# Loading a sum of positive parts over two DMA queues instead of one

## Chip, core and metric

The kernel runs on one core of a Trainium2 chip. The metric is the device time of one execution in microseconds (us), as the median of several runs. The core has the engines SyncE (SP, which issues DMAs), ScalarE (ACT), VectorE (DVE), GpSimd (POOL) and TensorE, which this kernel does not use. Data come from HBM through 16 DMA engines; a DMA instruction on an engine's own queue hands them their work.

## The reference

```python
x = randn(32, 512, 1024)            # float32, 67.1 MB
out = sum(maximum(x, 0), axis=-1)   # float32, 32 x 512
```

Each of 16,384 rows of 1024 numbers becomes one number, the sum of its positive parts. Every byte is read once and almost nothing is written.

## The kernel before

The rows are dealt to the 128 partitions. A **block** is 16 rows in each partition (128 x 16,384 floats, 8.39 MB), contiguous in HBM for each partition, so 64 KB in a piece. Seven blocks (0 to 6) go through three buffers `io0` to `io2` in turn; block 0 lies in a part of the input of its own, so that its sums can be stored early. An eighth block, the **tail**, comes in smaller and smaller loads: 8 rows, 4 rows, 2302 numbers ("head"), 873, 518 and 403 numbers, each partition. Before, all loads are issued by SyncE on its queue, by `load` (line 103). One load has one semaphore of its own, which counts 16 when it has landed.

Two ways of computing a row are used. For most blocks ScalarE clamps the whole block or half of it in place (`clamp`, line 144) and VectorE then reduces it along the last axis (`total`, line 152); `TWO` lists how many rows are taken at a time: 16 in blocks 0 and 1, twice 8 in blocks 2 to 4, twice 7 in block 5. The other rows are done alone, clamp and sum in one instruction with an accumulator, on ScalarE (`act_row`, line 159) or VectorE (`dve_row`, line 167); block 6 has eight of each, and the tail is done this way too, with the last two rows cut into parts (`act_part`, line 121, `dve_part`, line 126, a clamp on GpSimd, line 234, and a last joining instruction on VectorE, line 254).

The order on each engine is the order in which the program writes it; there is no scheduler. The first three loads wait for nothing. The load of block j from 3 on, and the first of the tail, waits until VectorE's count says that the block three before it, in the same buffer, has been read:

```python
loaded = load(buf[:, :, :], rows(m, ROWS), j >= NBUF and freed[j - NBUF])
```

`freed[j]` holds the counts of ScalarE and VectorE when block j is done; the load waits for VectorE's, which ends last. ScalarE's first instruction of block 0 is the load of its function table (line 142), which waits for block 0, and then the clamp. The three stores (line 115) are issued by SyncE behind all loads.

`open_without_barrier` takes the barrier out of the program's opening and puts the first load (`EARLY = 1`) ahead of the engine's first branch, so that it is issued at once.

Of the kernel before, what the change touches and what calls it, by code (L numbers as in the profile page):

```python
# [5 lines left out]
RELU = mybir.ActivationFunctionType.Relu  # L6
# [3 lines left out]
ROWS = 16  # L10
NBUF = 3
# [19 lines left out]
def kernel(tc: tile.TileContext, x: bass.AP, out: bass.AP):  # L31
    nc = tc.nc
    sems = Semaphores(tc)

    tc.close()
    tc.compile()
    nc.cur_bb = nc.bb_map[tc.start_bb_name]
    body = nc.cur_bb.bb.instructions
    ends = list(body)
    body.clear()  # L40
    n_stores = relu_sum(nc, sems, x, out)
    body.extend(ends)


    nc.cur_bb = nc.bb_map[tc.start_bb_name + "_end"]
    nc.cur_bb.bb.instructions.clear()
    nums = sorted(s.num for s in (*sems.loads, sems.act, sems.dve))
    cleared = range(nums[0], nums[-1] + 1)
    assert len(cleared) == len(nums)
    nc.sync.sem_clear(cleared)  # L50
    nc.sync.wait_ge(sems.stored, 16 * n_stores).then_inc(sems.stored, -16 * n_stores)
    open_without_barrier(tc, EARLY)
# [12 lines left out]
def relu_sum(nc, sems: Semaphores, x: bass.AP, out: bass.AP):  # L65
# [3 lines left out]
    NB = len(TWO)  # L69
# [4 lines left out]
    bufs = [nc.alloc_sbuf_tensor(f"io{i}", [P, ROWS, D], F32) for i in range(NBUF)]  # L74
    res = nc.alloc_sbuf_tensor("res", [P, NT], F32)
# [13 lines left out]
    def rows(m, n):  # L89
        if m < ROWS:  # L90
            return xf[:, m : m + n, :]
        return xv[:, m - ROWS : m - ROWS + n, :]
# [5 lines left out]

    n_load = n_act = n_dve = n_store = 0

    def load(dst, src, after=None):
        nonlocal n_load
        dma = nc.sync.dma_start(out=dst, in_=src)  # L103
        if after:
            dma.wait_op(sems.dve, after[1], "sem-ge")
        dma.then_inc(sems.loads[n_load], 16)
        n_load += 1
        return sems.loads[n_load - 1]

    def store(m, n, act, sem, count):  # L110
        nonlocal n_store
        dst, src = sums(m, n)
        if act:
            nc.sync.wait_ge(sems.act, act)
        nc.sync.dma_start(out=dst, in_=src).wait_op(sem, count, "sem-ge").then_inc(
            sems.stored, 16
        )
        n_store += 1
# [20 lines left out]
    def clamp(ap, loaded):  # L139
        nonlocal n_act  # L140
        if n_act == 0:
            nc.scalar.preload_act_table(RELU).wait_op(loaded, 16, "sem-ge")  # L142
            loaded = None
        i = nc.scalar.activation(out=ap, in_=ap, func=RELU)  # L144
        if loaded is not None:
            i.wait_op(loaded, 16, "sem-ge")
        i.then_inc(sems.act, 1)
        n_act += 1

    def total(ap, m, n):  # L150
        nonlocal n_dve
        nc.vector.tensor_reduce(  # L152
            out=res[:, m : m + n], in_=ap, axis=mybir.AxisListType.X, op=ADD
        ).wait_op(sems.act, n_act, "sem-ge").then_inc(sems.dve, 1)
        n_dve += 1

    def act_row(ap, accum_out, loaded):
        nonlocal n_act
        i = nc.scalar.activation(out=ap, in_=ap, func=RELU, accum_out=accum_out)  # L159
        if loaded is not None:  # L160
            i.wait_op(loaded, 16, "sem-ge")
        i.then_inc(sems.act, 1)
        n_act += 1

    def dve_row(ap, accum_out, loaded):
        nonlocal n_dve
        i = nc.vector.tensor_scalar(  # L167
            out=ap,
            in0=ap,
            scalar1=0.0,  # L170
            scalar2=None,
            op0=MAX,
            op1=ADD,
            accum_out=accum_out,
        )
        if loaded is not None:
            i.wait_op(loaded, 16, "sem-ge")
        i.then_inc(sems.dve, 1)
        n_dve += 1

    freed = []
    m = 0
    for j in range(NB):
        buf = bufs[j % NBUF]
        loaded = load(buf[:, :, :], rows(m, ROWS), j >= NBUF and freed[j - NBUF])
        c = 0
        act_waits = dve_waits = loaded
        for n in TWO[j]:
            clamp(buf[:, c : c + n, :], act_waits)
            total(buf[:, c : c + n, :], m + c, n)  # L190
            act_waits = None
            c += n
        for _ in range(ACT[j]):
            act_row(buf[:, c, :], res[:, m + c : m + c + 1], act_waits)
            act_waits = None
            c += 1
        for _ in range(DVE[j]):
            dve_row(buf[:, c, :], res[:, m + c : m + c + 1], dve_waits)
            dve_waits = None
            c += 1  # L200
        assert c == ROWS
        freed.append((n_act, n_dve))
        m += ROWS


    buf = bufs[NB % NBUF]
    c = 0
    for n in TAIL:
        loaded = load(
            buf[:, c : c + n, :], rows(m, n), None if c else freed[NB - NBUF]  # L210
        )
        for i in range(n):
            if i % 2 == 0 or (n == 8 and i == 7):
                act_row(buf[:, c, :], res[:, m : m + 1], loaded if i == 0 else None)
            else:
                dve_row(buf[:, c, :], res[:, m : m + 1], loaded if i == 1 else None)
            c += 1
            m += 1

    flat = buf[:, :, :].rearrange("p c d -> p (c d)")  # L220
    src = rows(m, 4).rearrange("p c d -> p (c d)")
    at = c * D
# [3 lines left out]


    loaded = load(flat[:, at : at + head], src[:, :head])
    act_row(buf[:, c, :], res[:, m : m + 1], loaded)
    sums_act = n_act  # L230
    dve_row(buf[:, c + 1, :], res[:, m + 1 : m + 2], loaded)
    sums_dve = n_dve
    clamped = flat[:, at + 2 * D : at + head]
    nc.gpsimd.tensor_scalar(  # L234
        out=clamped, in0=clamped, scalar1=0.0, scalar2=None, op0=MAX
    ).wait_op(loaded, 16, "sem-ge").then_inc(sems.end, 1)
    for lo, hi, n, first, second in (
# [3 lines left out]
        loaded = load(flat[:, at + lo : at + hi], src[:, lo:hi])  # L241
        act_part(flat[:, at + lo : at + lo + n], last[:, first : first + 1], (loaded, 16))
        dve_part(flat[:, at + lo + n : at + hi], last[:, second : second + 1], (loaded, 16))
    loaded = load(last[:, 2 : 2 + n_last], src[:, middle:end])
# [10 lines left out]
        out=clamped,  # L255
# [5 lines left out]
        accum_out=res[:, NT - 2 : NT - 1],  # L261
# [6 lines left out]
def open_without_barrier(tc: tile.TileContext, n_loads: int):  # L268

    SP = mybir.EngineType.SP
    blocks = tc.nc.main_func.blocks
    opening = blocks[0].instructions
    body = next(b for b in blocks if b.name == tc.start_bb_name).instructions
    for i in list(opening):
        if isinstance(i, (mybir.InstDrain, mybir.InstEventSemaphore)):
            opening.remove(i)
    loads = [i for i in body if i.engine == SP][:n_loads]
    for i in loads:  # L280
        assert isinstance(i, mybir.InstDMACopy)
        body.remove(i)
    at = next(n for n, i in enumerate(opening) if i.engine == SP)
    opening[at:at] = loads


# [28 lines left out]
```

## Time and profile before

| | before |
|---|---|
| median of 3 runs | 160.91 us (160.89 to 160.95) |
| span of the profiled execution, first to last instruction | 159.7 us |
| left around the span (median less span) | 1.2 us |
| VectorE busy | 118.8 us, 74% |
| ScalarE busy | 103.6 us, 65% |
| HBM read | 67.11 MB, 421 GB/s over the span |
| DMA queue's share of the 16 engines' time | 98.0% |

The whole time of the profiled execution isn't listed apart from the runs; its span is set beside their median. All windows and starts are counted from the span's start, which here is SyncE's first DMA instruction. In the timeline a line has start, length, engine, line of the program, operation, output and input, how many, and in brackets how long the engine was idle before it and what ended that. An engine's wait for `DMA io<-in_x_dram` ends when a load has landed, so the start of the first clamp of a block is the landing of that block, to within some hundredths of a microsecond. The chain of waits is followed back from the last instruction, at each step to what released it.

### The profile page before, as it was taken

Reading aid. Unit: us, or ns where it says so; the run is one execution under the profiler, and the core shown is the slowest. Engines: PE = TensorE matmul, PEld = TensorE weight load, DVE = VectorE, ACT = ScalarE, POOL = GpSimd, SP = SyncE. Lnnn points to the kernel's source line nnn. Section 1 sums busy time; section 2 is a strip of 40 time slices with the busy share of each in tenths; the row PEclk is TensorE's granted clock in tenths of the full one; section 3 lists DMA queues with packets and bytes.
Section 4 is the critical chain, followed back from the end, with each engine's and each line's share of the span. In section 5 each row is a group of like instructions: output and inputs, shape, how many; then the busy total and the mean of one; then the engine's idle time right before and its main releaser. Section 6 shows DMA issues by size and latency. Waiting matters only on the chain.

```text
span 159.7 us, 125 instructions
## 1 busy us (share of the span) xinstructions
DVE 118.8 (74%) x44; ACT 103.6 (65%) x53; POOL 1.0 (1%) x5
## 2 busy tenths in 40 slices
DVE  0000000006999799999999999999999799999986
ACT  0000049993699808996099951999329993496995
POOL 0000000000000000000000000000000000000001
DMA  7996996996997997979969969969969969898993
GB/s 263 525 525 263 525 509 279 525 509 279 525 476 312 525 443 345 525 328 460 525 279 509 525 263 525 525 263 525 509 279 525 492 295 525 353 435 386 407 409 128
DMA packets 2304, 67.18 MB, mean 421 GB/s; under 512 B 640, under 2 KB 768, under 8 KB 1024
## 3 DMA queue, kind: packets, MB, share of 16 engines
q1 hardware_dynamic: 2304, 67.18, 98.0%
HBM read 67.11 MB, written 0.07 MB: 421 GB/s over the span
## 4 chain that ended last, share of the span: by engine, by line
DVE 45%; DMA 45%; ACT 9%; SPq 1%; issue 0%
DMA io<-in_x_dram 45%; DVE res L152 43%; ACT io L144 9%; DVE io L167 1%; SPq L103 1%; DVE io L126 1%; DVE io L254 0%
## 5 line engine op out<-in xcount | busy, mean ns | idle before, releaser
L152 DVE TENSOR_REDUCE res<-io 128x8 f32<-128x8192 f32 (+2 forms) x10 | 101.1, 10175 | 38.9 <-ACT io L144 38.9
L144 ACT ACTIVATE io<-io 128x8192 f32<-128x8192 f32 (+2 forms) x10 | 81.8, 8218 | 25.9 <-DMA io<-in_x_dram 25.9
L159 ACT ACTIVATE io<-io 128x1024 f32<-128x1024 f32 x18 | 18.8, 1043 | 6.6 <-DMA io<-in_x_dram 6.6
L167 DVE TENSOR_SCALAR_CACHE_REDUCE io<-io 128x1024 f32<-128x1024 f32 x14 | 16.2, 1214 | 0.5 <-DMA io<-in_x_dram 0.4
L142 ACT ACT_TABLE_LOAD x1 | 1.3, 1283 | 22.0 <-DMA io<-in_x_dram 22.0
L159 ACT ACTIVATION_READ_ACCUMULATOR io<-io 128x1 f32 x18 | 3.4, 187 | 0.0
L234 POOL TENSOR_SCALAR io<-io 128x254 f32<-128x254 f32 x1 | 0.8, 840 | 155.1 <-DMA io<-in_x_dram 155.1
L167 DVE DVE_READ_ACCUMULATOR io<-io 128x1 f32 x14 | 1.1, 82 | 0.0
L126 DVE TENSOR_SCALAR_CACHE_REDUCE io<-io 128x552 f32<-128x552 f32 (+1 forms) x2 | 1.1, 596 | 0.0
L121 ACT ACTIVATE io<-io 128x321 f32<-128x321 f32 (+1 forms) x2 | 0.9, 426 | 0.1
L254 DVE SCALAR_TENSOR_TENSOR io<-last,io 128x254 f32<-128x254 f32 x1 | 0.4, 425 | 0.0
L121 ACT ACTIVATION_READ_ACCUMULATOR io<-io 128x1 f32 x2 | 0.4, 187 | 0.0
L121 ACT ACTIVATE last<-last 128x153 f32<-128x153 f32 x1 | 0.3, 332 | 0.0
L121 ACT ACTIVATION_READ_ACCUMULATOR last<-last 128x1 f32 x1 | 0.2, 187 | 0.0
L126 DVE DVE_READ_ACCUMULATOR io<-io 128x1 f32 x2 | 0.2, 84 | 0.0
L299 POOL MEMSET const-bfloat16-1.0<- 128x1 bf16 x1 | 0.1, 101 | 0.0
L299 POOL MEMSET const-uint8-127<- 128x1 uint8 x1 | 0.1, 101 | 0.0
L299 POOL MEMSET const-float32-0.0<- 128x1 f32 x1 | 0.1, 99 | 0.2 <-issue 0.2
L299 POOL MEMSET const-float32-1.0<- 128x1 f32 x1 | 0.1, 98 | 0.0
L254 DVE DVE_READ_ACCUMULATOR io<-last,io 128x1 f32 x1 | 0.1, 83 | 0.0
## 6 DMA issues: line engine op xcount, KB each, us to landing
io<-in_x_dram SPq DMA_DIRECT2D x1, 4096.0 KB, 23.8
io<-in_x_dram SPq DMA_DIRECT2D x1, 2048.0 KB, 28.3
io<-in_x_dram SPq DMA_DIRECT2D x1, 1151.0 KB, 30.6
io<-in_x_dram SPq DMA_DIRECT2D x1, 436.5 KB, 31.2
io<-in_x_dram SPq DMA_DIRECT2D x1, 259.0 KB, 31.4
last<-in_x_dram SPq DMA_DIRECT2D x1, 201.5 KB, 31.4
io<-in_x_dram SPq DMA_DIRECT2D x7, 29.1
out_dram<-res SPq DMA_DIRECT2D x1, 55.0 KB, 1.6
```

The lines of the kernel that those rows point to most:

```text
L103: dma = nc.sync.dma_start(out=dst, in_=src)
L121: nc.scalar.activation(out=ap, in_=ap, func=RELU, accum_out=accum_out).wait_op(*after, "sem-ge").then_inc(sems.end, 1)
L126: i = nc.vector.tensor_scalar(out=ap, in0=ap, scalar1=0.0, scalar2=None, op0=MAX, op1=ADD, accum_out=accum_out,)
L142: nc.scalar.preload_act_table(RELU).wait_op(loaded, 16, "sem-ge")
L144: i = nc.scalar.activation(out=ap, in_=ap, func=RELU)
L152: nc.vector.tensor_reduce(out=res[:, m : m + n], in_=ap, axis=mybir.AxisListType.X, op=ADD).wait_op(sems.act, n_act, "sem-ge").then_inc(se ...
L159: i = nc.scalar.activation(out=ap, in_=ap, func=RELU, accum_out=accum_out)
L167: i = nc.vector.tensor_scalar(out=ap, in0=ap, scalar1=0.0, scalar2=None, op0=MAX, op1=ADD, accum_out=accum_out,)
L234: nc.gpsimd.tensor_scalar(out=clamped, in0=clamped, scalar1=0.0, scalar2=None, op0=MAX).wait_op(loaded, 16, "sem-ge").then_inc(sems.end, 1)
L254: nc.vector.scalar_tensor_tensor(out=clamped, in0=last[:, : 2 + LAST_DVE], scalar=0.0, in1=clamped, op0=MAX, op1=ADD, accum_out=res[:, NT ...
L299: nc = _bacc.Bacc("TRN2", target_bir_lowering=False, num_devices=1)
```

## The change

Each of blocks 0 to 6 comes as two loads of eight rows, both counted on the block's one semaphore, and the consumers wait for 32 instead of 16. SyncE issues the first eight rows, at the place and with the wait that the whole block had. ScalarE issues the other eight rows on its own DMA queue: the three for blocks 0 to 2 at the start, the first of them ahead of its opening branch, and the one for block j + 1 (from 3 on) just ahead of block j's clamps in ScalarE's order, with the same wait for VectorE's count. The loads of the tail and the stores stay with SyncE, and the tail's loads still count 16.

```diff
+    def half(queue, j, first, after):
+        c = 0 if first else ROWS // 2
+        issue(
+            queue,
+            bufs[j % NBUF][:, c : c + ROWS // 2, :],
+            rows(j * ROWS + c, ROWS // 2),
+            sems.loads[j],
+            after,
+        )
...
-            nc.scalar.preload_act_table(RELU).wait_op(loaded, 16, "sem-ge")
+            nc.scalar.preload_act_table(RELU).wait_op(loaded, 32, "sem-ge")
...
-        loaded = load(buf[:, :, :], rows(m, ROWS), j >= NBUF and freed[j - NBUF])
+        half(nc.sync, j, True, j >= NBUF and freed[j - NBUF])
+        if j == 0:
+            for k in range(NBUF):
+                half(nc.scalar, k, False, None)
+        elif NBUF <= j + 1 < NB:
+            half(nc.scalar, j + 1, False, freed[j + 1 - NBUF])
+        loaded = sems.loads[j]
...
-    loads = [i for i in body if i.engine == SP][:n_loads]
...
+    for queue in queues:
+        loads = [i for i in body if i.engine == queue][:n_loads]
```

`issue` starts the DMA on the queue given, with the wait and a count of 16, as `load` did.

In each engine's order nothing else moves: VectorE, GpSimd and SyncE's later loads and stores have the instructions they had. SyncE's seven block loads are half as large, and ScalarE has seven DMA instructions more: three ahead of the table load, then one ahead of the clamps of blocks 2, 3, 4 and 5.

More of the change, by code (lines that the diff above doesn't have):

```diff
@@ L99, in relu_sum, with issue @@
     n_load = n_act = n_dve = n_store = 0
+    def issue(queue, dst, src, sem, after=None):
+        dma = queue.dma_start(out=dst, in_=src)
+        if after:
+            dma.wait_op(sems.dve, after[1], "sem-ge")
+        dma.then_inc(sem, 16)
     def load(dst, src, after=None):
         nonlocal n_load
[L103 to L106, printed above, removed]
+        issue(nc.sync, dst, src, sems.loads[n_load], after)
         n_load += 1
         return sems.loads[n_load - 1]
+    def half(queue, j, first, after):
[7 more added lines that the diff above has]
+        )
     def store(m, n, act, sem, count):
@@ L145, in clamp @@
         if loaded is not None:
-            i.wait_op(loaded, 16, "sem-ge")
+            i.wait_op(loaded, 32, "sem-ge")
         i.then_inc(sems.act, 1)
@@ L155, in total, with act_row @@
         n_dve += 1
-    def act_row(ap, accum_out, loaded):
+    def act_row(ap, accum_out, loaded, count=16):
         nonlocal n_act
@@ L160, in act_row, with dve_row @@
         if loaded is not None:
-            i.wait_op(loaded, 16, "sem-ge")
+            i.wait_op(loaded, count, "sem-ge")
         i.then_inc(sems.act, 1)
         n_act += 1
-    def dve_row(ap, accum_out, loaded):
+    def dve_row(ap, accum_out, loaded, count=16):
         nonlocal n_dve
@@ L176, in dve_row @@
         if loaded is not None:
-            i.wait_op(loaded, 16, "sem-ge")
+            i.wait_op(loaded, count, "sem-ge")
         i.then_inc(sems.dve, 1)
@@ L184, in relu_sum @@
         buf = bufs[j % NBUF]
-        loaded = load(buf[:, :, :], rows(m, ROWS), j >= NBUF and freed[j - NBUF])
+        half(nc.sync, j, True, j >= NBUF and freed[j - NBUF])
[5 more added lines that the diff above has]
+        loaded = sems.loads[j]
+        n_load = j + 1
         c = 0
@@ L193, in relu_sum @@
         for _ in range(ACT[j]):
-            act_row(buf[:, c, :], res[:, m + c : m + c + 1], act_waits)
+            act_row(buf[:, c, :], res[:, m + c : m + c + 1], act_waits, 32)
             act_waits = None
@@ L197, in relu_sum @@
         for _ in range(DVE[j]):
-            dve_row(buf[:, c, :], res[:, m + c : m + c + 1], dve_waits)
+            dve_row(buf[:, c, :], res[:, m + c : m + c + 1], dve_waits, 32)
             dve_waits = None
@@ L268, in open_without_barrier @@
 def open_without_barrier(tc: tile.TileContext, n_loads: int):
-    SP = mybir.EngineType.SP
+    queues = (mybir.EngineType.SP, mybir.EngineType.Activation)
     blocks = tc.nc.main_func.blocks
@@ L278, in open_without_barrier @@
             opening.remove(i)
-    loads = [i for i in body if i.engine == SP][:n_loads]
[L280 to L284, printed above, removed]
+    for queue in queues:
+        loads = [i for i in body if i.engine == queue][:n_loads]
+        for i in loads:
+            assert isinstance(i, mybir.InstDMACopy)
+            body.remove(i)
+        at = next(n for n, i in enumerate(opening) if i.engine == queue)
+        opening[at:at] = loads
 _INS = ['x']
```

## The prediction

> **What bounds the kernel now.** I read the page first (span, busy shares, queues), then the chain of waits, then the timeline for the moment at which each block lands, and last the trace's record of single transfers, for what a shorter one costs.
>
> ```profile
> span 159.7 us, 125 instructions
> DVE 118.8 (74%) x44; ACT 103.6 (65%) x53; POOL 1.0 (1%) x5
> q1 hardware_dynamic: 2304, 67.18, 98.0%
> HBM read 67.11 MB, written 0.07 MB: 421 GB/s over the span
> ```
>
> No compute engine is full, but the only DMA queue is: its packets take 98.0% of what 16 DMA engines have in the span. The chain of waits (start, length, what) says the same for both ends of the kernel:
>
> ```profile
> 0.43 40.86 DMA io<-in_x_dram
> 41.32 13.87 ACT io L144
> 55.21 68.79 DVE res L152 x7
> 124.87 30.59 DMA io<-in_x_dram
> 155.48 1.23 DVE io L167 x2
> ```
>
> The middle piece must not be read as "VectorE is the bound": it is only how the chain gets back to the moment when a buffer was freed. The timeline tells which wait is late there:
>
> ```profile
> 41.32 13.86 ACT L144 ACTIVATE io<-io 128x16384 f32<-128x16384 f32 x1 [4.18 <-DMA io<-in_x_dram]
> 60.67 13.95 ACT L144 ACTIVATE io<-io 128x8192 f32<-128x8192 f32 x2 [5.49 <-DMA io<-in_x_dram]
> 80.03 13.95 ACT L144 ACTIVATE io<-io 128x8192 f32<-128x8192 f32 x2 [5.42 <-DMA io<-in_x_dram]
> 99.38 13.95 ACT L144 ACTIVATE io<-io 128x8192 f32<-128x8192 f32 x2 [5.40 <-DMA io<-in_x_dram]
> 118.73 12.24 ACT L144 ACTIVATE io<-io 128x7168 f32<-128x7168 f32 x2 [5.40 <-DMA io<-in_x_dram]
> 124.94 15.15 DVE L152 TENSOR_REDUCE res<-io 128x7 f32<-128x7168 f32 x2 [0.95 <-ACT io L144]
> 138.08 1.06 ACT L159 ACTIVATE io<-io 128x1024 f32<-128x1024 f32 x1 [5.03 <-DMA io<-in_x_dram]
> 147.79 1.06 ACT L159 ACTIVATE io<-io 128x1024 f32<-128x1024 f32 x1 [1.29 <-DMA io<-in_x_dram]
> 155.48 1.22 DVE L167 TENSOR_SCALAR_CACHE_REDUCE io<-io 128x1024 f32<-128x1024 f32 x1 [0.42 <-DMA io<-in_x_dram]
> ```
>
> From 41.32 on, a block lands every 19.35 us (60.67, 80.03, 99.38, 118.73, 138.08) without exception. A block is 8.39 MB, so that is 433.5 GB/s, and the stream never pauses: the load that refills a buffer is issued when VectorE frees it, at 54.39 for block 3, about 72.4 for block 4, 89.6 for 5 and 106.8 for 6, always 5 to 12 us ahead of the landing before it. So the end is set by the bytes, the gaps between descriptors and the opening. VectorE is close behind: it is idle only 0.07 us before 152.69 and 0.42 us before 155.48, 0.5 us together after its last long reduce. I keep that slack for a rival.
>
> **The change, part by part.** The sum is made against the profiled execution, span 159.7 us; the median of the runs is 160.91, so 1.2 us lies around the span, and I take that as unchanged.
>
> *Removed and added transfers.* Seven loads of 8.39 MB become fourteen of 4.19 MB. The bytes, the order in memory if the two queues alternate, and everything after block 6 stay. In the trace's transfer records a block is eight descriptors of 64 KB on each DMA engine and a 4-byte completion write, and the 8-row tail load is eight of 32 KB and such a write. In steady state, from one start to the next, 64 KB takes 2414.5 ns, 32 KB 1209.5 ns, the completion write 6 ns. Before, a block is 8 x 2414.5 + 6 = 19,322 ns of an engine; after, 16 x 1209.5 + 2 x 6 = 19,364 ns. The difference is 42 ns a block, seven times that is 0.29 us. All of it lies on the path, since the path is the stream. The timeline bounds it from above: the 8-row load took 147.79 - 138.08 = 9.71 us, twice that is 19.42, 0.07 us over 19.35, and seven times that is 0.49. From below: if a second queue hid all gaps, the 42 ns would vanish and so would the gap in the 64 KB blocks (19,322 less twice the difference between 64 and 32 KB, 16 x 1205 = 19,280: again 42 ns), which makes -0.29 us. I take +0.29, because 32 KB descriptors back to back are the nearest thing to what will run.
>
> *Fourteen loads over two issuers.* SyncE keeps seven half loads and all tail loads at the same places, with the same waits, and its issue takes 0.33 to 0.47 us, idle time of that queue. Nothing to gain there: three loads are queued ahead at the start and one is always issued at least 5 us before it is needed. The Trainium skill, page "DMA: Bandwidth & Descriptors", section "Rules for kernel authors", says that spreading DMAs over issuing engines does not add bandwidth, because all share the same 16 DMA engines, and saves issue time only; the constant 433.5 GB/s on one queue agrees, and no term here hangs on it.
>
> *ScalarE's seven DMA instructions.* Its issue cost is not in the trace; I take SyncE's 0.33 to 0.47 us, as an estimate, and give it up to 1 us. Three come before the table load at 21.99, where ScalarE has nothing to do. The others stand between the clamps of one block and the wait for the next: for block 3 after the clamp of block 1 (free at 55.18, buffer freed at 54.39), for block 4 after block 2's clamps (about 74.6, against 72.4), for block 5 at 94.0 (89.6), for block 6 at 113.3 (106.8). Each of these waits is already met when ScalarE comes to it, and then it is idle for 5.40 to 5.49 us until the next landing. So both cost nothing. Queued behind each are the next block's clamps, and VectorE waits for those; without that cover 0.4 us per block would be added to VectorE's chain. The half load leaves 0.8 to 6.5 us later than SyncE's, but still some 5 us before its predecessor on the queue has landed, so that queue never runs empty either.
>
> *The doubled count (32 for 16)* has no duration of its own: the consumer starts when the later half lands.
>
> *The opening.* The first bytes move about 1.0 us after SyncE's first issue, and the first 64 KB descriptors take 2.8 to 3.3 us instead of 2.42, so 0.4 to 0.9 us of a cold start. ScalarE's first half load goes out in its own opening. Bounds: a gain of 0.8 us if its transfers fill that cold start, a loss of 0.4 us (one issue) if the two issuers delay each other's descriptors. I take nothing, as the bytes still need the same first read.
>
> Sum: 160.91 + 0.29 = 161.20 us.
>
> **Rivals.**
>
> *One queue slips a descriptor (slower).* If SyncE's queue has started its second descriptor on some DMA engine before ScalarE's first is there, and the queues then alternate, the SyncE half of every block finishes one descriptor early and the other half finishes 1.21 us late, behind the next block's first descriptor. The bytes end at the same time, but every block lands 1.21 us later, and block 5 with its 0.25 us from the sum 1.46 later than now. From there VectorE's chain (clamp, 15.15 us of reduces, the rows) has 0.50 us of slack, so the end moves by 0.96: 161.87 us. It decides once the lag of landings passes about 0.5 us. For it: ScalarE's start beside SyncE's is not in the trace, and the slowest of 16 engines counts. Against it: a first descriptor takes long enough to cover a skew of about 1 us. The Trainium skill, same page, section "Queues, rings and completion order", says that each DMA engine takes its queues in turn, packet by packet; no row here shows it, since all traffic is on q1. Chance 0.23.
>
> *Changing queues costs something.* Sixteen changes a block and seven blocks are 112; at 6 ns (the price of a completion write, the nearest row) that is 0.67 us, so 161.87; at 10 ns 162.3. Against: back-to-back descriptors leave about 4 ns now. Chance 0.09.
>
> *The opening is filled or the gaps are hidden (faster).* The 0.8 us of cold start makes 161.20 - 0.8 = 160.4; hidden gaps 160.91 - 0.29 = 160.62. For: two queues can have reads waiting at once. Against: 433.5 GB/s leaves little to hide. Chance 0.10.
>
> *The queues are served one after the other.* With three SyncE halves first, block 0 would be complete after four halves at about 41 instead of 22 us; VectorE's 118.8 us behind that gives some 175 us or more. Nothing speaks for it. Chance 0.02.
>
> That the change does nothing at all is the forecast's own neighbourhood: the two halves are the same bytes on the same engines.
>
> **How the numbers follow.** The forecast has 0.56. The measurement can tell about 0.2%, or 0.32 us, from no change, and 0.29 lies just inside; with the term's bounds from -0.29 to 0.49 and a few tenths for the opening I split it into 0.36 same, 0.18 slower, 0.02 faster. The slip, the queue change and serial service are slower (0.34), the filled opening mostly faster (0.09, with 0.01 same). Together: faster 0.11, same 0.37, slower 0.52. The forecast's own range is 160.9 to 161.5. The range to be scored goes up to 161.95 to hold the slip and the cheap end of the queue change, and down to 160.8; left out are most of the filled opening, the dear end of the queue change, and serial service.
>
> **What would show it.** Right: two hardware queues on the page; ScalarE's first clamps at 41.4, 60.8, 80.2, 99.6, 119.0 and 138.4, 19.39 us apart instead of 19.35; ScalarE still idle about 5 us before each, put down to DMA; the head load's row on VectorE at 155.77 after a short DMA wait. The slip: landings one step of about 1.2 us later from block 0 on with unchanged spacing, and no DMA wait left on VectorE before the head's row. Queue changes: spacing of 19.45 us or more. A filled opening: the table load before 21.9. The prediction is wrong if ScalarE's time before a clamp is put down to its own queue or to VectorE, or if the 19.35 us spacing shrinks.

## Result and profile after

| | before | after |
|---|---|---|
| median | 160.93 us (160.89 to 161.18) | 161.69 us (161.56 to 161.87) |
| ratio of the times | | 1.0047, 95% interval 1.0035 to 1.006 |
| span of the profiled execution | 159.7 us | 160.3 us |
| DMA queues | one | two |

The change makes the kernel slower by 0.76 us, just under half a per cent; the forecast was 161.20 in a range of 160.8 to 161.95. The page of the kernel after, its span, queues (packets, MB, share of the 16 engines' time) and HBM line:

```profile
span 160.3 us, 132 instructions
...
q1 hardware_dynamic: 2304, 37.82, 55.6%
q10 hardware_dynamic: 1008, 29.36, 42.5%
HBM read 67.11 MB, written 0.07 MB: 419 GB/s over the span
```

The work is divided over two queues, and the DMA engines are as full as with one (98.1% against 98.0%). The chain of waits shows the same stages as before; its two DMA pieces, 40.86 and 30.59 us in the kernel before, are now 41.10 and 30.86:

```profile
0.55 41.10 DMA io<-in_x_dram
41.66 13.87 ACT io L157
55.55 68.79 DVE res L165 x7
125.20 30.86 DMA io<-in_x_dram
156.09 1.23 DVE io L180 x2
```

The timeline of ScalarE, at its DMA instructions and at the landings:

```profile
0.12 1.35 ACTq L102 DMA_DIRECT2D io<-in_x_dram  x3
...
22.22 1.28 ACT L155 ACT_TABLE_LOAD   x1 [22.22 <-DMA io<-in_x_dram]
...
41.66 13.86 ACT L157 ACTIVATE io<-io 128x16384 f32<-128x16384 f32 x1 [4.29 <-DMA io<-in_x_dram]
54.66 0.36 ACTq L102 DMA_DIRECT2D io<-in_x_dram  x1
61.09 13.95 ACT L157 ACTIVATE io<-io 128x8192 f32<-128x8192 f32 x2 [5.57 <-DMA io<-in_x_dram]
72.80 0.36 ACTq L102 DMA_DIRECT2D io<-in_x_dram  x1
80.52 13.95 ACT L157 ACTIVATE io<-io 128x8192 f32<-128x8192 f32 x2 [5.48 <-DMA io<-in_x_dram]
...
138.82 1.06 ACT L172 ACTIVATE io<-io 128x1024 f32<-128x1024 f32 x1 [5.10 <-DMA io<-in_x_dram]
...
148.38 1.06 ACT L172 ACTIVATE io<-io 128x1024 f32<-128x1024 f32 x1 [1.14 <-DMA io<-in_x_dram]
```

Blocks land every 19.43 us (41.66, 61.09, 80.52, ... 138.82) where it was 19.35. No wait has changed its releaser: ScalarE still stands idle before each block for DMA, for about 5.5 us in mid-stream (4.29 before block 1, 5.10 before block 6). Two things more are to be read here. From block 6 to the tail's first load it is 9.56 us, less than the 9.71 before: the blocks' landings seem to carry something that the tail's don't. And the time rose by 0.76 us, the span of the profiled executions by only 0.6.

### The profile page after: what moved, and what is told of

Same layout as the page of the kernel before. It is cut to its first block, busy times and chain, and to the rows that moved or that the text cites. A ratio compares the mean times of both kernels' runs of the same rounds, so it can differ in the third digit from the quotient of the medians.

```text
span 160.3 us, 132 instructions
## 1 busy us (share of the span) xinstructions
DVE 118.7 (74%) x44; ACT 103.6 (65%) x53; POOL 1.0 (1%) x5
## 4 chain that ended last, share of the span: by engine, by line
DMA 45%; DVE 45%; ACT 9%; SPq 0%; ACTq 0%; issue 0%
DMA io<-in_x_dram 45%; DVE res L165 43%; ACT io L157 9%; DVE io L180 1%; DVE io L139 1%; SPq L102 0%; DVE io L274 0%; ACTq L102 0%
## 5 line engine op out<-in xcount | busy, mean ns | idle before, releaser
L180 DVE TENSOR_SCALAR_CACHE_REDUCE io<-io 128x1024 f32<-128x1024 f32 x14 | 16.2, 1214 | 0.4 <-DMA io<-in_x_dram 0.4
```

The lines of the kernel that those rows point to most:

```text
L180: i = nc.vector.tensor_scalar(out=ap, in0=ap, scalar1=0.0, scalar2=None, op0=MAX, op1=ADD, accum_out=accum_out,)
```

## Experiments

The ten kernels were timed in three groups, each beside the kernel before on one chip (its medians there: 160.97, 160.96 and 161.00 us). The time is the median of the runs. Spans are listed for every run to a tenth, so the mean over the runs is given; "time less span" is the mean time less the mean span, and in the kernel before it is 1.34, 1.35 and 1.33 us in the three groups. "A block" is the distance between the landings of two blocks in the profiled execution.

| kernel | time, us | ratio, 95% interval | mean span | time less span | a block, us |
|---|---|---|---|---|---|
| before (first group) | 160.97 | | 159.65 | 1.34 | 19.35 |
| changed kernel again | 161.68 | 1.0047 (1.0035 to 1.0059) | 160.24 | 1.49 | 19.43 |
| one_queue | 161.31 | 1.0022 (1.0013 to 1.0032) | 160.00 | 1.33 | 19.43 |
| block0_only | 161.22 | 1.0017 (1.0008 to 1.0026) | 159.67 | 1.56 | 19.35 |
| act_store | 161.13 | 1.0012 (1.0003 to 1.0021) | 159.63 | 1.53 | 19.35 |
| act_after_branch | 161.83 | 1.0055 (1.0041 to 1.007) | 160.24 | 1.55 | 19.43 |
| quarters_one | 162.40 | 1.0089 (1.0075 to 1.0102) | 161.03 | 1.36 | 19.58 |
| pieces_one_transfer | 161.34 | 1.0026 (1.0015 to 1.0037) | 160.06 | 1.35 | 19.43 |
| block0_one | 160.83 | 0.9991 (0.9982 to 0.9999) | 159.52 | 1.33 | 19.35 |
| block0_4_12 | 160.81 | 0.9992 (0.9983 to 1.0001) | 159.53 | 1.35 | 19.35 to 19.50 |
| part_halves | 302.06 | 1.8759 (1.8703 to 1.8815) | 300.40 | 1.55 | 39.4 |

**The changed kernel again.** 

> The changed kernel again, beside the others on the same chip. Both theories: +0.7 to +0.8 us over before, spacing 19.43 us; it shows how far these two numbers repeat.

161.68 us, the same to 0.01 us, with the same spacing.

**One queue for both halves.** SyncE issues both halves of every block, one behind the other.

```diff
-        if j == 0:
-            for k in range(NBUF):
-                half(nc.scalar, k, False, None)
-        elif NBUF <= j + 1 < NB:
-            half(nc.scalar, j + 1, False, freed[j + 1 - NBUF])
+        half(nc.sync, j, False, None)
...
```

> The changed kernel with both halves of every block issued by SyncE, one behind the other on its one queue; ScalarE issues nothing. In the changed kernel's trace a block lands every 19.43 us instead of 19.35 and the time rose by 0.76 us. Theory A (the pieces cost: every 32 KB descriptor costs the same extra wherever it is queued): spacing stays at 19.43, about +0.6 to +0.75 us over before. Theory B (the split alone costs what back-to-back 32 KB descriptors showed, 42 ns a block, and the rest comes from two queues taking turns): spacing 19.39, +0.25 to +0.35 us.

Its timeline, again the first clamps of blocks and the tail's first row:

```profile
21.76 1.28 ACT L155 ACT_TABLE_LOAD   x1 [21.76 <-DMA io<-in_x_dram]
...
41.19 13.86 ACT L157 ACTIVATE io<-io 128x16384 f32<-128x16384 f32 x1 [4.29 <-DMA io<-in_x_dram]
60.62 13.95 ACT L157 ACTIVATE io<-io 128x8192 f32<-128x8192 f32 x2 [5.58 <-DMA io<-in_x_dram]
...
138.33 1.06 ACT L172 ACTIVATE io<-io 128x1024 f32<-128x1024 f32 x1 [5.10 <-DMA io<-in_x_dram]
...
148.05 1.06 ACT L172 ACTIVATE io<-io 128x1024 f32<-128x1024 f32 x1 [1.30 <-DMA io<-in_x_dram]
...
155.74 1.06 ACT L172 ACTIVATE io<-io 128x1024 f32<-128x1024 f32 x1 [0.30 <-DMA io<-in_x_dram]
```

The answer is split. The spacing of 19.43 us is theory A's: the two queues taking turns cost nothing that one queue with the same pieces doesn't cost. The time of +0.34 us is in theory B's range, because in this kernel block 0 also lands earlier (at 21.76, not 22.22) and the time around the span stays at 1.33 us. So the changed kernel's loss has at least two parts. The 9.72 us from block 6 to the tail is here as before.

**Halves by partitions.**

```diff
-        c = 0 if first else ROWS // 2
+        p = 0 if first else P // 2
...
-            bufs[j % NBUF][:, c : c + ROWS // 2, :],
-            rows(j * ROWS + c, ROWS // 2),
+            bufs[j % NBUF][p : p + P // 2, :, :],
+            rows(j * ROWS, ROWS)[p : p + P // 2],
```

> Two queues as in the changed kernel, but a block is cut by partitions (64 and 64) and not by rows, so that descriptors stay 64 KB and their number per block stays that of before; only the number of transfers doubles. Theory A (the pieces cost): spacing back to 19.35 us, time within 0.1 us of before, plus at most 0.15 us for a later completion signal. Theory B (two queues taking turns cost): +0.35 to +0.5 us remains, spacing about 19.40.

Neither: 302 us. The page:

```profile
span 300.3 us, 132 instructions
...
q1 hardware_dynamic: 1856, 37.82, 52.9%
q10 hardware_dynamic: 560, 29.36, 46.1%
HBM read 67.11 MB, written 0.07 MB: 224 GB/s over the span
```

The engines are just as busy at half the rate: in the transfer records one 64 KB descriptor starts 4.93 us after another on an engine, instead of 2.41. The test couldn't tell the theories apart, because cutting by partitions brought in something much larger. The records show one thing that it changed: each engine takes its descriptors from the two queues in turn, and the engines do so nearly in step (95% of them, on the mean, are on the same queue), so at most moments nearly all write the same 64 partitions. That this is the cause is not shown. The Trainium skill, page "DMA: Bandwidth & Descriptors", section "Rules for kernel authors", says of two transfers to disjoint partition halves not to bother, since they serialize on the same engines; the run is far worse than that, and why was not tried.

**Only block 0 split over two queues.**

```diff
         if j == 0:
...
+            half(nc.sync, j, True, None)
+            half(nc.scalar, j, False, None)
+        else:
+            dma = nc.sync.dma_start(out=buf[:, :, :], in_=rows(m, ROWS))
...
```

> Only block 0 is split over the two queues; blocks 1 to 6 come whole on SyncE's queue, as before. It shows what the opening and the mere use of a second queue cost once. Theory A: one block's share, +0.08 us, spacing 19.35 us from block 1 on. Theory B with a cost that is paid once per program for the second queue (part of the 0.15 us by which the time rose more than the span): +0.15 to +0.3 us with spacing 19.35.

The span is that of before (159.67 against 159.65 us), the time 0.25 us more: what lies around the span rose from 1.34 to 1.56 us. That is a cost paid once, but it came in a kernel with another opening; hence the next.

**A second queue with almost no traffic.**

```diff
+        if j == NB - 1:
+            dst, src = sums(0, ROWS)
+            nc.scalar.dma_start(out=dst, in_=src).wait_op(
+                sems.dve, freed[0][1], "sem-ge"
+            ).then_inc(sems.stored, 16)
+            n_store += 1
...
-    store(0, ROWS, freed[0][0], sems.dve, freed[0][1])
```

> The kernel before, all loads whole on SyncE's queue; only the store of block 0's sums (8 KB) is issued by ScalarE on its own queue, behind block 5's work. Theory Q (a second queue in the program costs about 0.2 us once, outside the span): time less span rises from 1.33 to about 1.5 us, span within 0.1 us of before, time +0.15 to +0.3 us. Theory N (what lies around the span doesn't depend on the queues): time within 0.1 us of before.

```profile
span 159.6 us, 124 instructions
...
q1 hardware_dynamic: 2160, 67.17, 98.0%
q10 hardware_dynamic: 144, 0.01, 0.1%
```

Theory Q. With 0.01 MB on the second queue the span is unchanged (mean 159.63 in both) and the time less span goes from 1.35 to 1.53. So using ScalarE's queue at all costs this kernel about 0.18 us outside the span. The table says the same throughout: 1.49 to 1.56 us in the five rows with two queues, 1.33 to 1.36 in the six with one. What this time is spent on is not shown.

**Quarters on one queue.** Four loads of four rows for each block, all by SyncE; the consumers wait for 64:

```diff
+        for c in range(0, ROWS, 4):
+            issue(
+                nc.sync,
+                buf[:, c : c + 4, :],
+                rows(m + c, 4),
...
```

> Blocks 0 to 6 come as four loads of four rows (16 KB descriptors), all on SyncE's one queue; nothing on ScalarE's. Theory L (the stream goes at the pace at which pieces of that size land): before, the 4-row tail load took from 147.79 to 152.69 = 4.90 us, four times that is 19.60, so 0.22 to 0.25 us more a block than 19.35, spacing 19.57 to 19.60, +1.4 to +1.7 us in all, less up to 0.2 for an opening with smaller first pieces. Theory R (it goes at the pace of the transfer records, 607 ns for 16 KB): 32 x 607.3 + 4 x 6 = 19.46 us, 0.14 a block, +0.95 us.

```profile
41.63 13.86 ACT L157 ACTIVATE io<-io 128x16384 f32<-128x16384 f32 x1 [4.44 <-DMA io<-in_x_dram]
61.20 13.95 ACT L157 ACTIVATE io<-io 128x8192 f32<-128x8192 f32 x2 [5.72 <-DMA io<-in_x_dram]
80.78 13.95 ACT L157 ACTIVATE io<-io 128x8192 f32<-128x8192 f32 x2 [5.62 <-DMA io<-in_x_dram]
100.35 13.95 ACT L157 ACTIVATE io<-io 128x8192 f32<-128x8192 f32 x2 [5.62 <-DMA io<-in_x_dram]
```

Theory L: 19.57 to 19.59 us a block and +1.44 us. The stream goes at the pace at which pieces of that size landed in the tail of before, not at the closer pace of the transfer records. The extra is 0.08 us with 8 more descriptors on each engine and 0.23 us with 24 more, about 10 ns for each.

**Pieces without transfers.** Quarters change descriptors and transfers together. Here the load of each of blocks 1 to 6 is one transfer whose two halves come from rows 48 apart in HBM (so the sums leave in another order than the reference's):

```diff
-        loaded = load(buf[:, :, :], rows(m, ROWS), j >= NBUF and freed[j - NBUF])
+        dst, src = buf[:, :, :], rows(m, ROWS)
+        if j > 0:
+            dst = dst.rearrange("p (h k) d -> p h k d", h=2)
+            src = xv[:, : ROWS * (NB - 1), :].rearrange("p (h k) d -> p h k d", h=2)
+            src = src[:, :, 8 * (j - 1) : 8 * j, :]
+        loaded = load(dst, src, j >= NBUF and freed[j - NBUF])
```

> The kernel before with whole loads on one queue, but blocks 1 to 6 take their two halves from rows that are 48 rows apart in HBM, so that one transfer is made of 32 KB pieces: as many transfers and completions as before, as many descriptors as in the changed kernel. The sums of blocks 1 to 6 are stored in the order of the blocks and not of the rows. Theory D (the 0.08 us a block is paid for the descriptors): spacing 19.42 us, time +0.45 us. Theory T (it is paid for the second transfer and its completion): spacing 19.35, time within 0.1 us of before.

```profile
41.24 13.86 ACT L144 ACTIVATE io<-io 128x16384 f32<-128x16384 f32 x1 [4.28 <-DMA io<-in_x_dram]
60.66 13.95 ACT L144 ACTIVATE io<-io 128x8192 f32<-128x8192 f32 x2 [5.56 <-DMA io<-in_x_dram]
80.09 13.95 ACT L144 ACTIVATE io<-io 128x8192 f32<-128x8192 f32 x2 [5.48 <-DMA io<-in_x_dram]
```

Theory D: 19.42 to 19.44 us with one transfer and one completion a block. The price is paid for the number of descriptors. The time rose by 0.34 us for six split blocks, where 0.45 was expected; block 0, which is whole here as in the kernel before, landed at 21.81 us instead of 21.99, so openings differ by up to two tenths from one profiled execution to another.

**ScalarE's first load behind its branch.** `queues` in `open_without_barrier` holds SyncE alone.

> The changed kernel, but ScalarE's first half load stands behind its opening branch; SyncE's stays ahead of its own. The two-queue kernels had spans of 160.1 to 160.3 us, the one-queue kernel with the same pieces 159.9 to 160.1. Theory O (two issuers in the opening delay each other's first descriptors): span 159.9 to 160.1, time about 161.45. Theory P (the opening is not what differs): time 161.6 to 161.8 as with the changed kernel. If ScalarE's descriptors then miss SyncE's second ones, every block lands 1.2 us later and the time is about 162.3.

161.83 us, no better, as theory P has it. But ScalarE's first DMA starts at 0.13 us here and at 0.12 in the changed kernel, so the edit hardly moved what it was to move, and the opening stays open.

**Block 0 in two loads on one queue.** As `block0_only`, with `half(nc.sync, j, False, None)`.

> Only block 0 comes as two loads of eight rows, both on SyncE's queue; blocks 1 to 6 come whole. If smaller first pieces open the stream about 0.25 us earlier, as block 0's landing at 21.75 instead of 21.98 us in the one-queue kernel suggests, and one split block costs 0.08 us, the span is about 159.45 and the time 160.8, 0.1 to 0.2 us below before. If the opening was chance, +0.05 to +0.1 us.

160.83 against 160.96 us, 0.13 less, span 159.52 against 159.63: 0.09% faster. It is the one variant whose interval lies below 1, and that only just; as one of ten kernels tried, it is weak evidence of a gain.

**Block 0 as 4 and 12 rows.**

> Block 0 as two loads of 4 and 12 rows on SyncE's one queue, the rest whole. Block 0 in two halves on one queue gave 160.83 us against 160.96. If a shorter first piece is what opens the stream earlier, 16 KB does so a little more: 160.7 to 160.85 us, span 159.4 to 159.5; if it is only that a second transfer stands behind the first, the same as the halves, 160.8 to 160.9; if it was chance, 161.0.

160.81 against 161.00 us; its interval includes 1, and it can't be told from the halves. That a short first piece is what helps is not shown. (The uneven spacing in the table is from a profiled execution of 161.14 us, well above the median.)

## Why the prediction was right, and by how much it missed

The mechanism was right: the stream of bytes bounds the kernel, smaller pieces lengthen it block by block, and nothing on the compute engines changed. The sum was too small by 0.5 us, mostly in two terms. That the result lies in the range given is in part luck: 161.69 is above the forecast's own 160.9 to 161.5, and the range went up to 161.95 only to hold a slipped descriptor and a price for changing queues, neither of which happened. Of the chance of 0.52 for slower, 0.34 likewise stood on rivals that did not happen.

**"I take +0.29, because 32 KB descriptors back to back are the nearest thing to what will run."** This is the term that was mis-sized. I had two readings of the same 8-row load: 9.68 us by the transfer records (1209.5 ns a descriptor) and 9.71 by its landing, and took the former. Over whole blocks the latter holds: 19.43 - 19.35 = 0.08 us a block on two queues, on one queue, and with one transfer, 0.56 us for seven. The upper bound of the text, 0.49 us from 0.07 a block, was the better row, and even it was slightly exceeded. The records of the changed kernel show how a stretch of records can mislead: blocks 0 and 1 run at about 1209 ns a descriptor and those from block 2 on at 1213 to 1214, while block 1's landing is already 19.44 us behind block 0's in the timeline. The records were ahead of the landings and later fell to their pace; why is not shown.

**"1.2 us lies around the span, and I take that as unchanged."** This step failed. It grew by 0.15 us in the changed kernel (1.49 against 1.34), by 0.18 with a second queue that moves 0.01 MB. No row of before could show it, but a bound was owed. With it, 0.56 + 0.15 gives 0.71 us of the 0.71 to 0.76 measured. So the opening counts about nothing against before, as the text took it: block 0 landed 0.23 us later, of which 0.08 is its own descriptors and 0.15 the later counting told next, which does not reach the end.

**The doubled count** costs nothing by itself, as the one-queue kernel counts to 32 too; fed by two queues it has a price, but not at the end. In the transfer records the changed kernel's blocks land 0.53 to 0.60 us after SyncE's last completion write (ScalarE's last is within 0.01 us of it), the one-queue kernel's 0.36 to 0.46. The tail, on one queue, lands 0.44 to 0.47 us after its own and so gives the 0.15 us back, hence 9.56 instead of 9.71 us.

**The rivals.** The slipped descriptor did not happen: in the records each engine's first 32 KB comes from q1, its second from q10, and so on in turn to the end of block 6. That the queues are taken in turn agrees with the Trainium skill, page "DMA: Bandwidth & Descriptors", section "Queues, rings and completion order", which the prediction cites. The same sentence there has the turn last for a whole packet, typically about 9 to 17 descriptors; here it was one descriptor of 32 KB. ScalarE's first issue stood only 0.12 us behind SyncE's. Serial service is excluded by the same records, and the price for changing queues by the one-queue kernel's equal spacing. The opening was not filled: block 0 lands at 22.22 us, not earlier than 21.99.

**ScalarE's DMA instructions** took 0.36 to 0.45 us each and cost nothing, as said, but they did not leave when the text had it. It put them behind the clamps, at 55.2, 74.6, 94.0 and 113.3 us; they left at 54.66, 72.80, 89.99 and 107.17, within 0.01 us of SyncE's halves, as soon as VectorE had freed the buffer.

**VectorE** kept its slack: it waits for DMA for 0.45 us before the head's row, which the text had at 155.77.

```profile
156.09 1.22 DVE L180 TENSOR_SCALAR_CACHE_REDUCE io<-io 128x1024 f32<-128x1024 f32 x1 [0.45 <-DMA io<-in_x_dram]
```

Open: why the spans of the one-queue kernels are 0.15 to 0.24 us shorter (160.00 against 160.24 with all blocks split, 159.52 against 159.67 with block 0 alone). The transfer records show 0.10 to 0.17 us of it already in the first descriptor of each DMA engine: the earliest starts at 1.0 us in all of these kernels, but on the mean of the 16 engines the first 32 KB end at 2.94 and 2.95 us with one queue and at 3.05 to 3.11 with two.

## What to carry to other kernels

Where one queue already keeps the DMA engines at a constant rate, a second one brings no bytes sooner; count the descriptors that an edit adds, and price them by how far apart transfers of that size land, not by the records of a single transfer. Look at time less span as well as the span: a cost paid once per program, here for the second queue, is only seen there. Cut transfers along the rows and not across the partitions unless the run says otherwise.

## What the runs showed of the hardware that was not expected

- Two 64-partition transfers on two queues ran at 4.93 us for a 64 KB descriptor, half the rate of 128-partition transfers (2.41 us).
- A DMA instruction on ScalarE's queue does not wait until the computing instructions ahead of it have run. In the store experiment it stands behind block 5's clamps and rows, yet leaves 0.02 us after the first of them starts. It did not leave earlier either, though the count that it waits for was reached at 54.33 us, when SyncE's load with the same wait left:

```profile
118.64 6.18 ACT L144 ACTIVATE io<-io 128x7168 f32<-128x7168 f32 x1 [5.41 <-DMA io<-in_x_dram]
118.66 0.38 ACTq L188 DMA_DIRECT2D out_dram<-res  x1
```

- A block whose two halves come over two queues counts as landed about 0.15 us later than one whose halves come over one.
